# RWKV heads of a two-layer diffusion backbone: products within chunks over each head's own 64 rows, and one scan for the running sums of the decays

## The chip, the core and the metric

The kernel runs as one program on one core of a Trainium2 chip. The metric is the device time of one execution in microseconds (us), as the median of several runs. A second figure is the span of one profiled execution, from its first to its last instruction. The engines are called by the names of the profile: PE (TensorE, matrix products into PSUM), PEld (its weight loads), DVE (VectorE), ACT (ScalarE), POOL (GpSimd) and SP (the queue that issues the DMAs).

## What is computed

The reference is a backbone of two layers over 512 latent tokens and 256 context tokens, width 1024. Each layer is a mixer and an MLP with squared ReLU. The first mixer has GLA heads beside windowed attention, the second has eight RWKV-7 heads (64 wide, both directions of time) beside eight heads of latent attention (MLA). The change is in the RWKV heads of the second layer alone:

```python
def rwkv_scan(r, w, k, v, a, bb, s0):
    '''S_t = S_{t-1} (diag(w_t) + a_t b_t^T) + v_t k_t^T,  y_t = S_t r_t.'''
    def step(s, inp):
        r_t, w_t, k_t, v_t, a_t, b_t = inp
        sa = jnp.einsum('zbhij,zbhj->zbhi', s, a_t)
        s = s * w_t[..., None, :] + sa[..., :, None] * b_t[..., None, :] + v_t[..., :, None] * k_t[..., None, :]
        return s, jnp.einsum('zbhij,zbhj->zbhi', s, r_t)
...
y_ctx_d, s_ctx = rwkv_scan(*rwkv_dirs(f_ctx), s0)
y_lat_d, _ = rwkv_scan(*rwkv_dirs(f_lat), s_ctx)
```

Here f_ctx and f_lat are the features of the context and of the latents. The decay w is exp(-exp(w_log)) of a small projection; a is minus the normed key, b the normed key times a gate.

## The kernel before

**Chunks and lanes.** The kernel computes the recurrence by chunks of 64 tokens: 4 chunks of context, 8 of latents, taken in pairs p0 to p5 (p0 and p1 are the context). Everything lies by lanes: a lane is a direction and a pair of heads, so there are 8 lanes of 128 partitions, the first head on partitions 0 to 63, the second on 64 to 127 (`HALF`).

**Three stages run side by side**, as generators whose steps a plan interleaves (`plan`, L1787): `prep(p+2)` makes the operands and the products within a chunk, `inverse(p+1)` the triangular inverses, `chain(p)` the recurrence over the state. The plan's positions and priorities and the pools decide the order on each engine; each engine then works its own list in that order and waits on semaphores. Steps of `prep` for p0 and p1 stand among the MLA heads. In the trace the RWKV stage lies from 1334 to 1661 us, its pair of chunks that is looked at most closely, p4's `prep`, from 1526.40.

**prep** first makes the decays: products wz (L1549), exponentials on ACT into G, and then eight scans (L1563), one per lane, of 130 elements (two chunks of 65). The tile `reset` holds a zero at each chunk's start, so that the running sum begins anew. Per chunk, ACT makes the exponentials e1 and e3 (L1569, L1570). From these come the operands:

- AA (L1581), kk times e1, as 128x2x64 per lane: each head's rows in its own half of the columns, the other half zero (zeroed once), so that one product of 128 rows serves both heads. Four DVE writes of 64x256 a chunk.
- AC (L1585), the same values without zeros, two POOL writes of 128x256. It is transposed on PE (aT, L1601).
- BK (L1586), b and k times e3, two DVE writes of 128x512.
- RR (L1583), for latents only, r times e1 in the zero-padded form of AA: two DVE and two POOL writes of 64x256, with POOL memsets of the zero halves (L1576), since each chunk has a new RR.

The products within a chunk are gab (AA by BK, L1595), whose masked copy to GT is on DVE (L1596); the transposes aT and bkT, copied by ACT (GT L1605, BKT L1615); and for latents gmr (BK by RR, L1623), whose masked copy to GM is on DVE (L1625). Each is eight products of 128x128x128 over two PSUM banks, and each bank is copied as soon as its four products are done.

**inverse** ends in XT, which holds the inverses with zero halves, and gx (GT by XT, L1711), two banks a chunk, copied by ACT to GX (L1713).

**chain**: sa (GX by R, L1749), dS (L1760), S and R (L1763, L1765 on DVE), and for latents y, where S0 by RR (L1774) and R0 by GM (L1775) alternate into one bank.

The PSUM banks in this stage: 3 for prep (b), 2 for chain (c), 3 for inverse (i). An fp32 product shows in the trace as two hardware matmuls. Each wait is on the tile's last writer or reader.

Beside the last two recurrences run `gates` and `out1`, whose temporaries take the tags of pz (AA, G). After the stage the projection w_o follows: SP loads its weights into wraw (L335), ACT and DVE split them into whi and wlo (L322, L323), and SP also loads what the MLA heads left in DRAM (md) into the memory of actlo, and z (L1940).

Of the kernel before, what the change touches and what calls it, by code (L numbers as in the profile page):

```python
# [7 lines left out]
F32 = mybir.dt.float32  # L8
# [55 lines left out]
def _blocks(w):  # L64
    """[K, M] -> [M/128, 128 (k in tile), K/128, 128 (m in block)]"""
    k, m = w.shape
    return np.ascontiguousarray(w.reshape(k // P, P, m // P, P).transpose(2, 1, 0, 3))
# [18 lines left out]
def _rope_perm(half, reps):  # L86
    """lhsT of the signed swap: out[j] = sum_p m[p, j] x[p]; x1 rows get -x2, x2 rows get x1."""
# [12 lines left out]
class Pack:  # L100
    """columns of one [128, n] array, found by name"""
# [16 lines left out]
def prepare(i):  # L118
# [19 lines left out]
    # shape-only constants  # L138
# [20 lines left out]
    # modulation weights  # L159
    aw = i['ada_w']  # L160
    def outer(w):
        """[D, D] -> [128 (output in tile), tile, inner dimension]"""
        return w.reshape(D, KT, P).transpose(2, 1, 0)
# [5 lines left out]
    # layer 0 mixer  # L169
# [8 lines left out]
    # layer 1 mixer  # L178
# [54 lines left out]
def blocks(*ws):  # L233
    """the weights of each block of outputs, from parts of the inner dimension"""
# [3 lines left out]
class Act:  # L238
    """activations [128, KT, tokens], a tile for each part of the tokens; a slice of the tokens lies in one part"""
# [17 lines left out]
class Build:  # L257
# [6 lines left out]
    @contextmanager  # L264
    def prio(self, d):
        """what is issued inside stands d instructions later (earlier, if negative) in the scheduler's order"""
# [36 lines left out]
    def psum(self, b, s=0, **more):  # L303
        """PSUM as b single banks and s pairs of banks; more: banks of other tags. Tiles of a tag start in program
        order, so streams that run side by side have tags of their own"""
# [14 lines left out]
    def split(self, raw, hi, lo, eng=None):  # L320
        """raw = hi + lo exactly, both as float32r"""
# [3 lines left out]
    def weights(self, src, n=1024, keep=None, lead=PW):  # L325
        """one [128, n] block of weights from DRAM (or two halves of one), split"""
# [12 lines left out]
    def mm3(self, whi, wlo, ahi, alo, first, last, outs):  # L339
        """outs: list of (psum, slice of the moving operand); one k tile in three passes"""  # L340
# [8 lines left out]
    def dense(self, whi, wlo, hi, lo, nk, parts=PARTS):  # L349
        """[128 out, tokens] += w^T act; w [128, nk*128]; returns one psum tile per part"""  # L350
# [9 lines left out]
    def ada_first(self, pool, m0):  # L360
        """silu of the conditioning on all partitions, [128, stream, inner dimension]"""
# [25 lines left out]
    def ada_dot(self, pool, raw, ws, out):  # L387
        """out(w) = the weights [128, inner dimension] times the activation of stream w; raw is overwritten"""
# [4 lines left out]
    def ada_chunk(self, pool, l, j, among=False):  # L393
        """modulation part j of layer l, a tile of 128 outputs at a time: the weights with the inner dimension on
# [1635 lines left out]
```

## Time and profile before

| | |
|---|---|
| median of 3 runs | 2121.8 us (2116.98 to 2125.74) |
| span of the profiled execution | 2106.9 us |
| PE busy in it | 1976.5 us (94%) |
| DVE busy in it | 1391.4 us (66%) |
| ACT busy in it | 952.7 us (45%) |
| POOL busy in it | 308.6 us (15%) |

The profiled execution's own time isn't given beside its span; the median of the runs stands 14.9 us above the span. The shares are means over stages with different limits: most of PE's work is in the dense products of the projections and MLPs, and the share in the RWKV stage is read from that stretch alone. A busy PE is not a PE at its peak. Times in the rows are us from the span's start.

### The profile page before, as it was taken

Reading aid. Unit: us, or ns where it says so; the run is one execution under the profiler, and the core shown is the slowest. Engines: PE = TensorE matmul, PEld = TensorE weight load, DVE = VectorE, ACT = ScalarE, POOL = GpSimd, SP = SyncE. Lnnn points to the kernel's source line nnn. Section 1 sums busy time; section 2 is a strip of 40 time slices with the busy share of each in tenths; the row PEclk is TensorE's granted clock in tenths of the full one; section 3 lists DMA queues with packets and bytes.
Section 4 is the critical chain, followed back from the end, with each engine's and each line's share of the span. In section 5 each row is a group of like instructions: output and inputs, shape, how many; then the busy total and the mean of one; then the engine's idle time right before and its main releaser. Section 6 shows DMA issues by size and latency. Waiting matters only on the chain. (4 is left out here: it accounts for less than half of the span.)

```text
span 2106.9 us, 35640 instructions
## 1 busy us (share of the span) xinstructions
PE 1976.5 (94%) x14304; PEld 1643.3 (78%) x14304; DVE 1391.4 (66%) x2574; ACT 952.7 (45%) x1835; POOL 308.6 (15%) x517
## 2 busy tenths in 40 slices
PE   8998999989899999999989999978888899999998
PEld 6877666667788888888878877767677797888887
DVE  8775898736897656534484558878887555444454
ACT  5426676544622222222255646765654535333332
POOL 0003455301200000000021020033342011000001
PEclk9999799999999999999999999998999899999999
DMA  8650000053354554312243100000001412332241
GB/s 298 202 161 14 1 2 1 1 180 102 114 183 134 158 160 145 117 60 93 88 150 113 41 1 6 9 9 2 3 2 33 132 59 85 108 103 90 90 136 41
DMA packets 66282, 180.38 MB, mean 86 GB/s; under 512 B 7235, under 2 KB 12099, under 8 KB 65989
## 3 DMA queue, kind: packets, MB, share of 16 engines
q1 hardware_dynamic: 66116, 178.11, 26.4%
q8 instruction: 112, 1.84, 0.4%
q14 instruction: 54, 0.43, 0.1%
HBM read 172.57 MB, written 5.51 MB: 85 GB/s over the span
## 5 line engine op out<-in xcount | busy, mean ns | idle before, releaser
L322 ACT CAST whi<-wraw 128x1024 fp32r<-128x1024 f32 (+2 forms) x253 | 221.4, 878 | 641.2 <-PE mm L345 565.8
L343 PE MATMUL mm<-acthi,whi 128*128 128x512 f32 (+1 forms) x1464 | 443.4, 349 | 12.9 <-ACT whi L322 12.2
L347 PE MATMUL mm<-acthi,wlo 128*128 128x512 f32 (+1 forms) x1464 | 438.9, 346 | 9.3 <-DVE wlo L323 9.2
L345 PE MATMUL mm<-actlo,whi 128*128 128x512 f32 (+1 forms) x1464 | 442.2, 348 | 2.6 <-POOL actlo L1085 2.5
L323 DVE TENSOR_TENSOR wlo<-wraw,whi 128x1024 fp32r<-128x1024 f32 (+2 forms) x253 | 257.1, 1019 | 218.6 <-ACT whi L322 214.2
L343 PEld LDWEIGHTS mm<-acthi,whi 128*128 128x128 f32 x1464 | 250.7, 191 | 51.3 <-ACT whi L322 14.9
L347 PEld LDWEIGHTS mm<-acthi,wlo 128*128 128x128 f32 x1464 | 251.4, 192 | 49.0 <-DVE wlo L323 13.2
L345 PEld LDWEIGHTS mm<-actlo,whi 128*128 128x128 f32 x1464 | 251.0, 191 | 39.8 <-POOL actlo L1085 3.9
L347 PE MATMUL mm<-hh,wlo 128*128 128x512 f32 (+1 forms) x832 | 252.8, 341 | 3.6 <-DVE wlo L323 3.6
L343 PE MATMUL mm<-hh,whi 128*128 128x512 f32 (+1 forms) x832 | 253.7, 342 | 0.0
L345 PE MATMUL mm<-hl,whi 128*128 128x512 f32 (+1 forms) x832 | 253.3, 342 | 0.1
L1085 POOL TENSOR_TENSOR actlo<-lnu,acthi 128x256 fp32r<-128x256 f32 (+1 forms) x48 | 60.3, 1271 | 717.4 <-DVE lnu L1083 630.4
L347 PEld LDWEIGHTS mm<-hh,wlo 128*128 128x128 f32 x832 | 143.9, 189 | 23.2 <-DVE wlo L323 4.2
L345 PEld LDWEIGHTS mm<-hl,whi 128*128 128x128 f32 x832 | 143.6, 189 | 19.2 <-issue 0.7
L343 PEld LDWEIGHTS mm<-hh,whi 128*128 128x128 f32 x832 | 143.1, 189 | 19.5 <-issue 1.0
L1157 DVE SCALAR_TENSOR_TENSOR z<-mm,mod,z 128x512 f32<-128x512 f32 (+1 forms) x144 | 94.0, 659 | 96.6 <-PE mm L347 96.3
L391 DVE SCALAR_TENSOR_TENSOR araw<-araw,scb 128x1024 f32<-128x1024 f32 x80 | 97.8, 1222 | 56.4 <-DMA araw<-in_ada_r_dram 55.6
L1011 DVE SCALAR_TENSOR_TENSOR z<-mm,mod,z 128x256 f32<-128x256 f32 (+1 forms) x64 | 34.9, 548 | 81.2 <-PE mm L347 79.6
L322 ACT CAST hh<-relu 128x512 fp32r<-128x512 f32 (+1 forms) x100 | 50.4, 534 | 79.5 <-DVE relu L1109 79.5
L615 POOL TENSOR_TENSOR lk<-kd,Dt 64x128 f32<-64x128 f32 x144 | 74.5, 517 | 48.5 <-ACT Dt L597 20.0
L323 DVE TENSOR_TENSOR hl<-relu,hh 128x512 fp32r<-128x512 f32 (+1 forms) x100 | 56.1, 587 | 26.5 <-ACT hh L322 26.1
L391 DVE SCALAR_TENSOR_TENSOR aprod<-araw,scb 128x1024 bf16<-128x1024 f32 x48 | 58.5, 1220 | 19.6 <-DMA araw<-in_ada_r_dram 19.6
(465 smaller groups left out, 3394.0 us busy)
## 6 DMA issues: line engine op xcount, KB each, us to landing
araw<-in_ada_r_dram SPq DMA_DIRECT2D x80, 512.0 KB, 3.8
wraw<-in_w_dram SPq DMA_DIRECT2D x72, 512.0 KB, 3.5
wraw<-in_w_dram SPq DMA_DIRECT2D x144, 256.0 KB, 2.6
wraw<-in_w_s_dram SPq DMA_DIRECT2D x31, 512.0 KB, 3.6
wraw<-in_w_o_dram SPq DMA_DIRECT2D x22, 512.0 KB, 3.6
scraw<-in_ada_sc_dram SPq DMA_DIRECT2D x8, 512.0 KB, 5.3
shraw<-in_ada_sh_dram SPq DMA_DIRECT2D x8, 512.0 KB, 5.7
x<-in_xT_dram SPq DMA_DIRECT2D x8, 384.0 KB, 5.7
```

The costliest lines, as they stand in the source:

```text
L322: self.nc.scalar.copy(hi, raw)
L323: (eng or self.nc.vector).tensor_tensor(lo, raw, hi.bitcast(F32), op=ALU.subtract)
L343: mm(o, whi, ahi[:, sl], start=first, stop=False)
L345: mm(o, whi, alo[:, sl], start=False, stop=False)
L347: mm(o, wlo, ahi[:, sl], start=False, stop=last)
L391: self.nc.vector.scalar_tensor_tensor(pr, raw, 1.0, self.scb[:, w], op0=ALU.mult, op1=ALU.mult, accum_out=out(w))
L615: nc.gpsimd.tensor_tensor(K[r, :, x], kk[r, :, x], d[r, :, x], op=ALU.mult)
L1011: nc.vector.scalar_tensor_tensor(zs, o, self.mod[:, l, self.wh(i, parts), g, d:d + 1], zs, op0=ALU.mult, op1=ALU.add)
L1085: eng.tensor_tensor(lo[:, k, sl], u, hi[:, k, sl].bitcast(F32), op=ALU.subtract)
L1157: nc.vector.scalar_tensor_tensor(z[:, d, sl], o, self.mod[:, l, self.wh(i, parts), 5, d:d + 1], z[:, d, sl], op0=ALU.mult, op1=ALU.add)
```

## The change

All lines of commentary go. Line numbers shift by up to ten. What is computed differently:

- The eight scans become one over all 1040 elements of G, with `reset` as long.
- AA goes. AC is written by DVE (two writes of 128x256 a chunk) and serves gab as well as aT. RR has no zero halves: two DVE writes of 128x256, no POOL writes, no memsets. XT has no zero halves.
- gab is 16 products a chunk: for each lane and head the diagonal 64x64 tile, AC's 64 columns stationary, 128 columns of BK moving.
- gmr and gx are 16 products a chunk: 64 rows of one head, 128 stationary columns, 64 moving columns, the two heads into two banks by turns. Both banks are opened before the first product, and each is copied (GM by DVE, GX by ACT) when all have been issued.
- y first adds up all products of S0 by RR, now as 64x64 diagonal tiles, and then all of R0 by GM; the start flag stands at the first lane, the stop flag at the last.
- The temporaries of `out1` take AC's tag and not AA's; the raw tile of w_o in `gates` has 1024 columns.

```diff
-        reset = pz.tile([P, 130], F32, name="reset")
+        reset = pz.tile([P, 8 * 130], F32, name="reset")
...
-        AA = zeroed(pz, [P, 8, 2, 64], "AA")
...
-            for j in range(8):
-                gj = G[:, j].rearrange("p c t -> p (c t)")
-                nc.vector.tensor_tensor_scan(gj, reset, gj, 0.0, op0=ALU.mult, op1=ALU.add)
+            gj = G.rearrange("p j c t -> p (j c t)")
+            nc.vector.tensor_tensor_scan(gj, reset, gj, 0.0, op0=ALU.mult, op1=ALU.add)
...
-                RR = r2.tile([P, 8, 2, 64], F32, name="RR", bufs=BKB) if lat else None
-                if lat:
-                    for h in range(2):
-                        nc.gpsimd.memset(RR[HALF[h], :, 1 - h], 0.0)
+                RR = r2.tile([P, 8, 64], F32, name="RR", bufs=BKB) if lat else None
                 for d in range(2):
                     L = slice(d * 4, d * 4 + 4)
-                    for h in range(2):
-                        r = HALF[h]
-                        nc.vector.tensor_tensor(AA[r, L, h], nat('kk', d, cc)[r], e1[r, L, 0:64], op=ALU.mult)
-                        if lat:
-                            (nc.gpsimd if d else nc.vector).tensor_tensor(RR[r, L, h], nat('r', d, cc)[r], e1[r, L, 1:65],
-                                                                          op=ALU.mult)
-                    nc.gpsimd.tensor_tensor(AC[:, L], nat('kk', d, cc), e1[:, L, 0:64], op=ALU.mult)
+                    nc.vector.tensor_tensor(AC[:, L], nat('kk', d, cc), e1[:, L, 0:64], op=ALU.mult)
                     nc.vector.tensor_tensor(BK[:, L], nat('kb', d, cc),
                                             e3[:, L].unsqueeze(2).to_broadcast([P, 4, 2, 64]), op=ALU.mult)
-                kb = lambda j: BK[:, j].rearrange("p a t -> p (a t)")
+                    if lat:
+                        nc.vector.tensor_tensor(RR[:, L], nat('r', d, cc), e1[:, L, 1:65], op=ALU.mult)
+                kb = lambda j, r=slice(0, P): BK[r, j].rearrange("p a t -> p (a t)")
...
-                        mm(gp[:, u], AA[:, jb * 4 + u].rearrange("p a t -> p (a t)"), BK[:, jb * 4 + u, ::-1], start=True, stop=True)
+                        for r in HALF:
+                            mm(gp[r, u], AC[r, jb * 4 + u], BK[r, jb * 4 + u, ::-1], start=True, stop=True)
...
-                    for jb in range(2):
-                        gp = self.bank("gmr")
-                        for u in range(4):
-                            mm(gp[:, u * P:u * P + P], kb(jb * 4 + u), RR[:, jb * 4 + u].rearrange("p a t -> p (a t)"),
-                               start=True, stop=True)
-                        nc.vector.tensor_tensor(GM[:, jb * 4:jb * 4 + 4], gp.rearrange("p (j h t) -> p j h t", j=4, h=2),
-                                                self.k2('up').unsqueeze(1).unsqueeze(1).to_broadcast([P, 4, 2, 64]), op=ALU.mult)
+                    gp = [self.bank("gmr") for _ in HALF]
+                    for j in range(8):
+                        for o, r in zip(gp, HALF):
+                            mm(o[:, j * 64:j * 64 + 64], kb(j, r), RR[r, j], start=True, stop=True)
+                    for h, o in enumerate(gp):
+                        nc.vector.tensor_tensor(GM[:, :, h], o.rearrange("p (j t) -> p j t", j=8),
+                                                self.k2('up').unsqueeze(1).to_broadcast([P, 8, 64]), op=ALU.mult)
...
-                for jb in range(2):
-                    gp = self.bank("gx", "i")
-                    for u in range(4):
-                        j = jb * 4 + u
-                        mm(gp[:, u * P:u * P + P], GT[:, j, 1:3].rearrange("p a t -> p (a t)"),
-                           XT[:, c * 8 + j].rearrange("p a t -> p (a t)"), start=True, stop=True)
-                    nc.scalar.copy(GX[:, jb * 4:jb * 4 + 4].rearrange("p j h t -> p (j h t)"), gp)
+                gp = [self.bank("gx", "i") for _ in HALF]
+                for j in range(8):
+                    for o, r in zip(gp, HALF):
+                        mm(o[:, j * 64:j * 64 + 64], GT[r, j, 1:3].rearrange("p a t -> p (a t)"), XT[r, c * 8 + j],
+                           start=True, stop=True)
+                for h, o in enumerate(gp):
+                    nc.scalar.copy(GX[:, :, h], o.rearrange("p (j t) -> p j t", j=8))
...
                     for j in range(8):
-                        for h in range(2):
-                            r = HALF[h]
-                            o = yp[r, j * 64:j * 64 + 64]
-                            mm(o, S0[:, j], RR[:, j, h], start=True, stop=False)
-                            mm(o, R0[:, j, h], GM[:, j, h], start=False, stop=True)
+                        for r in HALF:
+                            mm(yp[r, j * 64:j * 64 + 64], S0[r, j], RR[r, j], start=(j == 0), stop=False)
+                    for j in range(8):
+                        for h, r in enumerate(HALF):
+                            mm(yp[r, j * 64:j * 64 + 64], R0[:, j, h], GM[:, j, h], start=False, stop=(j == 7))
...
-                    XT = zeroed(rp, [P, 16, 2, 64], "XT")
+                    XT = zeroed(rp, [P, 16, 64], "XT")
```

The order of the instructions on the engines moves with it. On DVE, the start of p4's `prep`, before: the scans, the operands of the first chunk with the recurrence's S and R between them, and the first GT.

```order
L1563 SCALAR_TENSOR_TENSOR G<-reset,G 128x130 x8
L1581 TENSOR_TENSOR AA<-fl_kk,e_14461 64x4x64
L1583 TENSOR_TENSOR RR<-fl_r,e_14461 64x4x64
L1763 TENSOR_TENSOR S<-dS,S 128x512
L1581 TENSOR_TENSOR AA<-fl_kk,e_14461 64x4x64
L1765 TENSOR_TENSOR R<-S,PC 64x8x64 x2
L1583 TENSOR_TENSOR RR<-fl_r,e_14461 64x4x64
L1586 TENSOR_TENSOR BK<-fl_kb,e_14462 128x512
L1581 TENSOR_TENSOR AA<-fl_kk,e_14461 64x4x64 x2
L1586 TENSOR_TENSOR BK<-fl_kb,e_14462 128x512
L1596 TENSOR_TENSOR GT<-gab,con_10197 128x4x128
```

The same place after. A row with x2 stands for two instructions; e is e1 or e3.

```order
L1560 SCALAR_TENSOR_TENSOR G<-reset,G 128x1040
L1573 TENSOR_TENSOR AC<-fl_kk,e_14520 128x256
L1577 TENSOR_TENSOR RR<-fl_r,e_14520 128x256
L1573 TENSOR_TENSOR AC<-fl_kk,e_14520 128x256
L1755 TENSOR_TENSOR S<-dS,S 128x512
L1574 TENSOR_TENSOR BK<-fl_kb,e_14521 128x512
L1757 TENSOR_TENSOR R<-S,PC 64x8x64 x2
L1574 TENSOR_TENSOR BK<-fl_kb,e_14521 128x512
L1577 TENSOR_TENSOR RR<-fl_r,e_14520 128x256
L1587 TENSOR_TENSOR GT<-gab,con_10197 128x4x128 x2
```

Eight operand writes and eight scans ahead of the first GT have become six writes and one scan, and the first BK, which stood behind R, stands ahead of it.

On PE, the rest of p4's first chunk, before. The order counts an fp32 product as one; xt and xn are products of the `inverse` of p3.

```order
L1595 MATMUL gab<-BK,AA 128x128 x4
L1601 MATMUL aT<-col,AC 128x128 x4
L1614 MATMUL bkT<-col,BK 128x128 x4
L1670 MATMUL xt_14700<-V,DT 32x32 x4
L1614 MATMUL bkT<-col,BK 128x128 x4
L1670 MATMUL xt_14700<-V,DT 32x32 x6
L1623 MATMUL gmr<-RR,BK 128x128 x4
L1670 MATMUL xt_14700<-V,DT 32x32 x6
L1623 MATMUL gmr<-RR,BK 128x128 x4
L1670 MATMUL xt_14700<-V,DT 32x32 x37
L1595 MATMUL gab<-BK,AA 128x128 x4
```

The same place after.

```order
L1586 MATMUL gab<-BK,AC 64x128 x8
L1592 MATMUL aT<-col,AC 128x128 x4
L1605 MATMUL bkT<-col,BK 128x128 x8
L1662 MATMUL xt_14759<-V,DT 32x32 x21
L1615 MATMUL gmr<-RR,BK 128x64 x8
L1662 MATMUL xt_14759<-V,DT 32x32 x4
L1615 MATMUL gmr<-RR,BK 128x64 x8
L1662 MATMUL xt_14759<-V,DT 32x32 x39
L1586 MATMUL gab<-BK,AC 64x128 x8
```

The second half of gmr stood behind six products of xt and each half had a copy of its own; now 16 products, with four of xt between them, end before the first copy.

On PE, the end of `inverse` for p3 and the recurrence that reads it, before.

```order
L1711 MATMUL gx<-XT,GT 128x128 x8
L1749 MATMUL sa<-R,GX 64x64 x8
L1728 MATMUL vT<-col,fl_v 64x128 x2
L1749 MATMUL sa<-R,GX 64x64 x8
L1728 MATMUL vT<-col,fl_v 64x128 x2
L1711 MATMUL gx<-XT,GT 128x128 x5
L1728 MATMUL vT<-col,vr 64x128 x4
L1711 MATMUL gx<-XT,GT 128x128 x3
L1760 MATMUL dS<-R,BKT 64x64 x16
```

The same place after.

```order
L1702 MATMUL gx<-XT,GT 128x64 x21
L1741 MATMUL sa<-R,GX 64x64
L1720 MATMUL vT<-col,fl_v 64x128 x3
L1741 MATMUL sa<-R,GX 64x64 x15
L1720 MATMUL vT<-col,fl_v 64x128
L1702 MATMUL gx<-XT,GT 128x64 x9
L1720 MATMUL vT<-col,vr 64x128 x4
L1702 MATMUL gx<-XT,GT 128x64 x2
L1752 MATMUL dS<-R,BKT 64x64 x16
```

The first chunk's gx now is 16 products, and 5 of the second chunk's stand ahead of sa; two of gx stand behind the transposes vT, right ahead of dS.

On SP, one load of wraw from w_o now stands ahead of the eight loads of md into actlo, where all six stood behind them, and two loads of z that stood behind the md loads stand ahead.

## Rows read from the trace of the kernel before

**Rows 1.** Busy time by stretch: us, engines with instructions, granted PE clock, DMA share.

```profile
1334.00:1437.00 103.00, 85.89 (x1005) 70.44 (x1003) 87.06 (x179) 67.24 (x131) 25.58 (x43) 0.92 0.03 8
...
1521.00:1564.50 43.50, 38.17 (x844) 33.31 (x843) 36.44 (x71) 24.42 (x52) 16.53 (x27) 0.92 0.01 3
```

**Rows 2.** DVE in order of time, p4's turn: start, duration, [idle before <-releaser].

```profile
1526.40 2.77 DVE L1563 TENSOR_TENSOR_SCAN G<-reset,G 128x130 f32<-128x130 f32 x8
1529.96 0.42 DVE L1581 TENSOR_TENSOR AA<-fl_kk,e 64x256 f32<-64x256 f32 x1 [0.79 <-ACT e L1569]
...
1534.73 1.42 DVE L1586 TENSOR_TENSOR BK<-fl_kb,e 128x512 f32<-128x512 f32 x1
...
1543.44 0.69 DVE L1625 TENSOR_TENSOR GM<-gmr,con 128x512 f32<-128x512 f32 x1 [0.61 <-PE gmr L1623]
...
1549.18 0.69 DVE L1596 TENSOR_TENSOR GT<-gab,con 128x512 f32<-128x512 f32 x1
...
1563.95 0.68 DVE L1763 TENSOR_TENSOR S<-dS,S 128x512 f32<-128x512 f32 x1
```

**Rows 3.** PE in order of time, the same turn.

```profile
1536.20 1.16 PE L1595 MATMUL gab<-BK,AA 128*128 128x128 f32 x8 [1.84 <-DVE BK L1586]
...
1539.25 1.06 PE L1601 MATMUL aT<-col,AC 128*128 128x128 f32 x4
...
1542.24 1.16 PE L1623 MATMUL gmr<-RR,BK 128*128 128x128 f32 x8
...
1561.72 1.15 PE L1760 MATMUL dS<-R,BKT 128*64 128x64 f32 x32
```

**Rows 4.** ACT in order of time, the same turn.

```profile
1540.35 1.50 ACT L1605 COPY GT<-aT 64x256 f32<-64x256 f32 x4 [1.96 <-PE aT L1601]
...
1542.71 1.07 ACT L1615 COPY BKT<-bkT 128x512 f32<-128x512 f32 x2
```

**Rows 5.** DVE groups, 1366 to 1660: busy us, mean ns of one, idle before.

```profile
L1581 DVE TENSOR_TENSOR AA<-fl_kk,e 64x256 f32<-64x256 f32 x32 | 17.7, 554 | 2.3 <-ACT e L1569 1.8
...
L1586 DVE TENSOR_TENSOR BK<-fl_kb,e 128x512 f32<-128x512 f32 x16 | 14.0, 873 | 0.2
L1563 DVE TENSOR_TENSOR_SCAN G<-reset,G 128x130 f32<-128x130 f32 x40 | 13.6, 416 | 2.3 <-ACT G L1559 2.3
...
L1583 DVE TENSOR_TENSOR RR<-fl_r,e 64x256 f32<-64x256 f32 x16 | 10.9, 683 | 0.1
...
L1581 DVE TENSOR_TENSOR AA<-fx_kk,e 64x256 f32<-64x256 f32 x12 | 6.4, 530 | 0.1
...
L1784 DVE TENSOR_TENSOR Y<-Y,y 128x256 f32<-128x256 f32 x8 | 3.0, 416 | 1.4 <-PE y L1775 1.3
```

**Rows 6.** POOL groups of the same stretch.

```profile
L1585 POOL TENSOR_TENSOR AC<-fl_kk,e 128x256 f32<-128x256 f32 x16 | 13.6, 858 | 2.2 <-PE aT L1601 1.8
```

**Rows 7.** PE in order of time: three shapes of product, and two shapes by turns.

```profile
1546.52 1.20 PE L1676 MATMUL xn<-DT,V 32*32 32x32 f32 x64
...
1562.80 0.70 PE L1549 MATMUL wz<-tz,con 128*128 128x256 f32 x2
1563.43 0.33 PE L1774 MATMUL y<-RR,S 128*64 128x64 f32 x2
1563.69 0.70 PE L1549 MATMUL wz<-tz,con 128*128 128x256 f32 x2
...
1567.84 1.15 PE L1749 MATMUL sa<-R,GX 128*64 128x64 f32 x31
```

**Rows 8.** PE in order of time near the start: products with two moving columns.

```profile
21.00 1.84 PE L440 MATMUL sh<-scc,shraw 128*128 128x2 f32 x16
```

**Rows 9.** All engines in order of time, the start of the w_o projection.

```profile
1661.57 3.99 SPq L1940 DMA_DIRECT2D actlo<-md  x8
...
1673.38 1.22 DVE L323 TENSOR_TENSOR wlo<-wraw,whi 128x1024 fp32r<-128x1024 f32 x1
...
1674.75 0.58 PE L343 MATMUL mm<-acthi,whi 128*128 128x256 f32 x1 [1.43 <-ACT whi L322]
```

More of the change, by code (lines that the diff above doesn't have):

```diff
@@ L1691, in inverse @@
                 b = (q % 2) * 32
-                (nc.gpsimd.tensor_copy if q < 2 else nc.scalar.copy)(XT[QD[q], :, q // 2, b:b + 32], XD[QD[q]])
+                (nc.gpsimd.tensor_copy if q < 2 else nc.scalar.copy)(XT[QD[q], :, b:b + 32], XD[QD[q]])
             yield
@@ L1700, in inverse @@
                 r = QD[2 * h]
-                nc.scalar.copy(XT[r, :, h, 32:64], g3(xo[r]))
+                nc.scalar.copy(XT[r, :, 32:64], g3(xo[r]))
             yield
@@ L1837, in gates @@
         for d, (src,) in enumerate(blocks(self.a['w1_o'])[:2]):
-            raw = rp.tile([P, 1536], F32, tag="BK", name="woraw")[:, 0:1024]
+            raw = rp.tile([P, 1024], F32, tag="BK", name="woraw")
             nc.sync.dma_start(raw, src)
@@ L1907, in layer1 @@
                 tmp = lambda tag, shape: lambda: pz.tile([P, shape], F32, tag=tag, name="g" + tag)[:, 0:512]
-                chunks = self.rwkv(pz, pools(), (self.gates(pz), self.out1(0, tmp("AA", 1024), tmp("G", 1040))))
+                chunks = self.rwkv(pz, pools(), (self.gates(pz), self.out1(0, tmp("AC", 512), tmp("G", 1040))))
                 with tc.tile_pool(name="ml", bufs=1, reuse_waits="tile") as ml:
```

## Prediction

> **What bounds the kernel now.** I first read the table of busy time by stretch [rows 1]. In the stretch from 1521.00 to 1564.50, one whole turn of the RWKV stage, PE works 38.17 of 43.50 us and VectorE 36.44: neither is full, so the turn is a chain that goes from one engine to the other, and only work on that chain counts. The rows in order of time tell which way it goes. VectorE runs the eight scans from 1526.40, ScalarE's exponentials end at 1529.96, then VectorE builds the operands until BK ends at 1536.15 [rows 2]. PE stands idle for 1.84 us until then and starts gab at 1536.20 [rows 3]. Then aT at 1539.25, its copies on ScalarE [rows 4], gmr, the second chunk's products, and the last masked copy GT at 1549.18 [rows 2]; the inverse of the next turn needs that GT, and the next scans come 45 us after these. So the operand writes of the first chunk are on the chain and those of the second (up to 1542.8) lie beside PE work.
>
> The profiled span is 2106.9 us; the median of the three runs is 2121.8. I add the difference, 14.9, to a predicted span.
>
> **Operand writes and scans.** Per chunk of latents, VectorE's four AA writes of 554 ns [rows 5] become two AC writes of 128x256, the size of the sum into Y that takes 416 ns [rows 5]; its two RR writes of 683 ns become two of 416, and GpSimd's share goes: two AC writes of 858 ns [rows 6], two of RR and two of zeros. For a pair of chunks that is VectorE 2 x (4 x 0.554 - 2 x 0.416) = 2.8 us and 2 x 2 x (0.683 - 0.416) = 1.1 us less. BK averages 873 ns, though the same shape and source took 1.42 us at 1534.73 while GpSimd was busy, and GM, of the same size, 0.69; I take 0.68 without GpSimd at its side, 4 x 0.19 = 0.8 less. Eight scans of 130 elements, 2.77 us issued one behind the other, become one of 1040. What is fixed in one scan isn't shown here: at nothing fixed it stays 2.8 us, and if all of a short scan but a rate of one 128x256 write (416 ns for 256, 1.6 ns an element) were fixed, it is 1.7. I take 2.35, the nearer to the row, so -0.4. Together -5.1 us of VectorE work in a pair, of which the first chunk's half and the scan are on the chain.
>
> Laid out from the scan's start s = 1526.40 in the order of the changed program: scan to s+2.35, exponentials, AC at s+3.1, RR, AC, the state's sum (it comes where it came, s+4.2), BK to s+5.7, the two R to about s+7.5, BK to s+8.2, and gab's second half behind it: aT at s+8.9 in place of s+12.85 [rows 3]. **Gain 3.95 us.**
>
> **The products.** For gab eight pairs of 64x64 diagonal tiles take the place of eight full products. A row of n matmuls lasts n pitches and some 0.2 us, by which the last one's record is longer. A full 128x128 product is two hardware matmuls of 0.11 us (gab: eight in 1.16 [rows 3]). Diagonal tiles run side by side: 32x32 ones of xn show 64 matmuls in 1.20 us, 16 ns each [rows 7]. So the two halves should share the time of one, and gab's PE time stays. In gmr and gx each of 16 products has 64 rows, 128 columns of weights and 64 moving columns. Moved alone, 64 columns need half of 0.11 us; the column halves of sa show 31 matmuls in 1.15 us, 31 ns each [rows 7]. The weights are the question: with two moving columns only, sixteen 128x128 matmuls take 1.84 us [rows 8], so a 128-column weight load alone is 0.10 to 0.11 us. If the two row halves load side by side, a matmul costs 0.055 and PE time stays as it is; if they don't, 0.11, and gmr and gx cost twice as much. I take 0.055, since the 32-row strips of xn seem to load theirs side by side (below, B), and keep the other end below.
>
> In y the S0 products become 64x64 diagonals and stand ahead of the R0 products. The alternation of two products in y runs at some 30 ns a matmul now, so nothing is won there, and between full-size products it costs: wz 0.70, y 0.33, wz again start 0.89 us apart [rows 7], some 0.35 above the work of both. The changed order has gab cut once into y, and 37 such changes of shape in a pair against 38: nothing.
>
> **What is given back.** gmr now opens two banks before its first product, and its sixteen products must end before either GM can start. The stage has three banks for these tags. The second gmr bank is the one that the first BKT copy leaves, at t0+4.0 (t0 is aT's start; BKT at 1542.71, half of 1.07 us [rows 4]). So gmr starts at t0+4.1 instead of t0+3.0, takes 32 x 0.055 plus a piece of xt and two changes of shape, 2.45 us, and ends at t0+6.55, where the second GM of before could start at t0+5.5. Both GM, both BK, DT, GT and two DT stand behind it on VectorE, the waiting engine: 8 operations of 0.6 to 0.7 us put the last GT at t0+11.6; before it stood at t0+9.93 [rows 2, 3]. **Loss 1.65 us.**
>
> gx has the same form: both copies GX come after all sixteen products. sa and dS then stand 0.9 us later, and dS ended at 1562.87 while S waited for VectorE until 1563.95 [rows 2, 3]: 1.1 us of cover, so nothing; without it, 0.9 a chunk.
>
> So a pair of latent chunks gains 3.95 - 1.65 = 2.3, and the four of them 9.2. **The context pairs** run among MLA heads, where PE is busy 85.89 of 103.00 us [rows 1]: VectorE saves 4 x (4 x 0.530 - 2 x 0.416) = 5.2 us there (AA from fx_kk [rows 5]) and 0.8 in scans; I take half of it on the path, -2.9, and +1.0 for gab's pieces among full-size products (nine places, 0.35 each, a third on the path): -1.9. **The tail** of the last pair has one gx with nothing beside it: +0.5.
>
> **The loads at the end.** Before, eight actlo loads of md wait on SP's queue until 1661.57 for VectorE's last read of the temporary beneath them, and the w_o weights stand behind them [rows 9]. In the changed layout they lie elsewhere: the order has the first w_o load ahead of the md loads, and none of them waits for that read any more. It is worth nothing, since PE's idle 1.43 us at 1674.75 ends with VectorE's wlo, which stands at 1673.38 behind Y's gating and the sum into z of the block before [rows 9]; if PE waits for the load alone, 2 us go.
>
> **Sum:** -9.2 - 1.9 + 0.5 = -10.6, a span of 2096.3 and **2111.2 us**. Its own range is 2103 to 2120: all of the context savings (3), a scan of 1.7 (2.6) and the loads (2) make it 8 less; no context gain (1.9) and no cover for gx (4 x 2 x 0.9) make it 9 more.
>
> **Rivals.** (B, slower) The halves' weights load one after the other: 0.11 us a matmul [rows 8]. gmr then takes 32 x 0.055 = 1.8 us more a chunk, all of it ahead of GM and, in the second chunk, of gx; gx takes 1.8 more a chunk, against which 0.2 of cover is left. A pair goes from -2.3 to -2.3 + 4 x 1.8 - 0.2 = +4.7, the four to +18.8, the tail to 0.5 + 3.6; with -1.9 that is +21, **2143**. It decides from about 73 ns a matmul, where a third of these 32 us uses up the gain of 10.6. For it: the weights are 128 columns wide, whatever the rows. The Trainium skill ("TensorE: Matmul & The Clock Gate", LDWEIGHTS) says that a weight load takes time by columns and not by rows, which by itself would give this. Against it stand the 16 ns of the 32-row strips [rows 7]: a load of 32 columns, a quarter of 0.10 us, would take 26 ns, and loads one after the other wouldn't fit. The same page (Part 3, The mechanism) lets a load overlap a running matmul when the row groups differ, which is the case here.
>
> (C, larger gain) PE's clock: the mean granted in the turn is 0.92 and in the first stretch too [rows 1], so the lower level, 1.2 GHz, was granted in some 16% of the time, 7 us of a turn; ahead of gab PE had stood idle for 1.84 us [rows 3]. With gab 4 us earlier some of that goes, and if GM's delay meets idle time, the loss above goes too: 1.65 x 4 + 2 = 9 more, **2102**, at best 2095.
>
> (D, no change) The 64x64 diagonals don't run side by side: gab's 32 half matmuls a chunk cost 0.11 us each and not 0.055, 1.6 us more after the overlap at their ends, and a pair's gain of 2.3 becomes a loss of 0.9: 4 x 0.9 - 1.9 + 0.5 = +2, **2124**. Against it: the strips of xn.
>
> **How the numbers follow.** Forecast 0.50, B 0.20, C 0.20, D 0.10. Forecast is 2111; the range reaches from 2096 (C) to 2139 (most of B); it leaves out C's end and B's upper half. Half a per cent, 10.6 us, is about what a measurement of this kernel can tell from no change; the forecast lies on that bound. Faster: C and nearly half of the forecast, 0.42. Same: the rest of the forecast and D with a little of B, 0.38. Slower: B, 0.20.
>
> **What would show it.** One scan row of 2.2 to 2.5 us; AC at 0.42 and BK at 0.68; first gab 5.7 us after the scan's start, aT 9 after it; gmr 1.8 us for 32 matmuls (B: 3.5); last GT 11.6 after aT; dS done before S is free for it; scans 42 to 43 us apart instead of 45. It would be wrong if gmr or gx take over 75 ns a matmul, if y's split costs a clock fall, or if the period of the scans is held by the inverse alone and doesn't move.

## The result, and the profile after

The changed kernel takes 2140.9 us (median of four runs, 2128.42 to 2149.73); the kernel before, timed with it, takes 2122.7 (four runs, 2116.98 to 2125.74). The ratio is 1.0101, with a 95% interval of 1.0073 to 1.0129: slower by 1.0%. The forecast was 2111.2, faster by 0.5%; the range ended at 2139.0.

The profiled execution of after has a span of 2133.7 us and a mean granted clock of 0.953. I cut both traces at the same events: the start of the first pair's scans, that of the third pair's (p2), that of the last (p5), and the first product of w_o. The first stretch is the context's, among the MLA heads; the second holds three turns of the latents; the third the last turn and the tail. Columns are as in [rows 1]. Before:

```profile
1334.08:1441.78 107.70, 88.72 (x1041) 72.78 (x1039) 89.34 (x183) 70.06 (x135) 26.62 (x44) 0.91 0.03 8
1441.78:1571.35 129.57, 109.28 (x2363) 94.53 (x2361) 111.87 (x219) 75.68 (x160) 48.24 (x75) 0.92 0.01 3
1571.35:1662.89 91.54, 79.40 (x1618) 63.06 (x1619) 59.55 (x120) 42.01 (x79) 20.23 (x29) 0.90 0.14 40
```

After:

```profile
1341.58:1455.31 113.73, 99.71 (x1180) 79.20 (x1181) 84.16 (x161) 69.56 (x136) 15.32 (x29) 0.85 0.03 7
1455.31:1593.58 138.27, 127.24 (x2619) 109.88 (x2605) 101.53 (x186) 73.64 (x157) 26.08 (x45) 0.86 0.01 2
1593.58:1687.86 94.28, 84.74 (x1754) 68.83 (x1755) 56.57 (x109) 43.72 (x82) 12.69 (x19) 0.89 0.21 62
```

The stage grew from 328.8 to 346.3 us, by 17.5, which is about the whole difference of the medians (18.2). One profiled execution of each is not a sharp measure, though: their spans differ by 26.8 us, and 7.5 of these lie ahead of the stage, where nothing was changed. POOL's and DVE's work shrank in all three stretches, as the change says (DVE 111.87 to 101.53 in the three turns). PE's grew from 109.28 to 127.24 us there, and its granted clock fell from 0.92 to 0.86; in the context stretch it fell from 0.91 to 0.85. So the time came in on PE, by work and by clock. The context stretch has no gmr, and e1 and e5 below, with the same products in it, run it in 108.50 and 107.34 us; so some 5 of its 113.73 us are chance of this one execution, and the three turns are the part to read.

p4's turn, engine by engine. DVE in order of time, the answer to [rows 2]:

```profile
1547.83 2.33 DVE L1560 TENSOR_TENSOR_SCAN G<-reset,G 128x1040 f32<-128x1040 f32 x1 [0.58 <-ACT G L1557]
1550.92 0.42 DVE L1573 TENSOR_TENSOR AC<-fl_kk,e 128x256 f32<-128x256 f32 x1 [0.77 <-ACT e L1566]
...
1552.54 0.68 DVE L1574 TENSOR_TENSOR BK<-fl_kb,e 128x512 f32<-128x512 f32 x1
...
1569.78 0.69 DVE L1587 TENSOR_TENSOR GT<-gab,con 128x512 f32<-128x512 f32 x1 [0.52 <-PE gab L1586]
1575.67 1.97 DVE L1631 STREAM_TRANSPOSE X<-TA 128x1024 f32<-128x1024 f32 x1 [5.20 <-PE x L1690]
```

PE in order of time, the answer to [rows 3], with gmr of both chunks and gx:

```profile
1553.31 1.09 PE L1586 MATMUL gab<-BK,AC 64*64 64x128 f32 x16
...
1556.43 0.66 PE L1592 MATMUL aT<-col,AC 128*128 128x128 f32 x4
...
1559.25 2.00 PE L1615 MATMUL gmr<-RR,BK 64*128 64x64 f32 x16 [0.30 <-ACT GT L1596]
...
1561.37 2.00 PE L1615 MATMUL gmr<-RR,BK 64*128 64x64 f32 x16
...
1564.09 1.90 PE L1586 MATMUL gab<-BK,AC 64*64 64x128 f32 x16
1565.92 1.91 PE L1668 MATMUL xn<-DT,V 32*32 32x32 f32 x64
...
1575.46 2.05 PE L1615 MATMUL gmr<-RR,BK 64*128 64x64 f32 x30
...
1577.52 2.84 PE L1702 MATMUL gx<-XT,GT 64*128 64x64 f32 x40
...
1582.30 1.77 PE L1702 MATMUL gx<-XT,GT 64*128 64x64 f32 x18
```

And the same turn cut into four stretches, columns as in [rows 1]:

```profile
1547.83:1559.25 11.42, 9.90 (x237) 7.94 (x237) 10.57 (x16) 7.60 (x18) 3.67 (x7) 1.00 0.01 3
1559.25:1564.20 4.95, 4.95 (x120) 4.73 (x122) 2.41 (x5) 1.85 (x4) 0.00 (x0) 1.00 0.00 0
1564.20:1574.40 10.20, 10.20 (x178) 9.08 (x180) 3.84 (x6) 4.25 (x9) 2.00 (x4) 0.50 0.01 3
1574.40:1593.58 19.18, 18.84 (x410) 16.04 (x408) 16.77 (x37) 11.55 (x25) 2.96 (x4) 1.00 0.01 3
```

The first half of the turn went as predicted: AC 3.1 us after the scan's start, the first BK done at 5.4, aT at 8.6 (12.85 before). Then three things are to be seen. gmr of the first chunk is two rows of 16 matmuls with 2.00 us each, 115 ns from start to start (a single record of this shape lasts 0.27 us, which is taken off for the last one); in the second chunk 30 matmuls take 2.05 us, 61 ns. From 1559.25 on PE has no idle time, 4.95 of 4.95 us and 10.20 of 10.20. In the kernel before, too, it had next to none behind aT; it waited ahead of it, as the same turn shows there (scan to aT, and from aT to behind the last GT):

```profile
1526.40:1539.25 12.85, 8.75 (x186) 7.89 (x183) 11.89 (x23) 5.22 (x11) 7.67 (x12) 0.82 0.01 1
1539.25:1553.00 13.75, 13.42 (x356) 11.89 (x355) 9.38 (x15) 7.57 (x18) 4.84 (x10) 0.92 0.02 4
```

So PE's work behind aT had little room to grow. And from 1564.20 for 10.2 us the granted clock is 0.50, the lower of the two levels (1.2 GHz), with PE busy without a gap ahead of it: gab takes 1.90 us there and 1.09 at 1553.31. VectorE now waits 5.20 us for PE ahead of X.

Why 115 and 61 ns: the order of the changed program, with the numbers of the tiles, which the words of the plain order hide.

```order
L1615 MATMUL gmr_14653<-RR_14526,BK_11885 128x64 x8
L1662 MATMUL xt32_14759<-V_14744,DT_14676 32x32 x4
L1615 MATMUL gmr_14654<-RR_14526,BK_11885 128x64 x8
```

The two numbers are the two banks, one for each head. The loop writes the heads by turns, but when it comes up the second bank isn't free, and in the order that is built all of the first head stands ahead of all of the second; it is so in the first chunk of all four latent pairs. In the second chunks the heads alternate, in p3 from the first product on, in the others behind three to five products of each head.

### The profile page after: what moved, and what is told of

Read it like the earlier page. It is cut to its first block, busy times and chain, and to the rows that moved or that the text cites. A ratio compares the mean times of both kernels' runs of the same rounds, so it can differ in the third digit from the quotient of the medians.

```text
span 2133.7 us, 36522 instructions
## 1 busy us (share of the span) xinstructions
PE 2018.6 (95%) x14816; PEld 1675.7 (79%) x14816; DVE 1374.4 (64%) x2508; ACT 951.9 (45%) x1835; POOL 265.5 (12%) x460
## 4 chain that ended last, share of the span: by engine, by line
PE 75%; DVE 13%; ACT 5%; DMA 4%; issue 3%; POOL 1%; DVEq 0%; SPq 0%; ACTq 0%; POOLq 0%
PE mm L345 17%; PE mm L347 17%; PE mm L343 16%; DMA araw<-in_ada_r_dram 3%; PE var L1053 2%; PE go L786 2%; PE ms L1435 1%; DVE wlo L323 1%; PE gx L1702 1%; PE gab L1586 1%; PE gmr L1615 1%; PE lev L660 1%; DVE z L1069 1%; PE st L1479 1%; DVE araw L391 1%
```

## Experiments

The theories. **T1**: the loss comes from products of half of the rows that don't alternate: they take 0.11 us and not 0.055, and PE's clock falls behind them. **T2**: the tiles of 64 rows lower the clock as such, alternating or not. **T3**: the place of gmr behind bkT is what costs. **T4**: gx carries the loss. **T5**: any longer gmr lowers the clock through the waits of others. All runs, with the stage measured as above in the one profiled execution, the granted clock in the three turns of its middle stretch, and the ratio to the kernel before from the timed runs:

```
kernel                              stage us  clock  median us  ratio to before (95%)
before                              328.8     0.92
after                               346.3     0.86   2140.9     1.0101 (1.0073 to 1.0129)
e1  gmr ahead of bkT                321.8     0.96   2117.8     0.9993 (0.9964 to 1.0021)
e2  full gmr                        -         -      2116.7     0.9984 (0.9957 to 1.0011)
e3  full gmr and gx                 314.4     0.97   2091.7     0.9878 (0.9855 to 0.9902)
e4  writes alone                    317.1     0.94   2093.6     0.9895 (0.9865 to 0.9926)
e5  e1, one head after the other    355.2     0.85   2162.6     1.0211 (1.0169 to 1.0253)
e6  e1 with gx of before            320.7     0.92   2105.8     0.9946 (0.9922 to 0.9971)
e7  after with gx of before         334.9     0.87   2118.1     1.0018 (1.0001 to 1.0036)
e8  before with gmr ahead of bkT    328.2     0.89   2119.6     1.0019 (1.0000 to 1.0038)
e9  e1, full gmr issued twice       342.8     0.96   2120.4     1.0009 (0.9980 to 1.0038)
e10 put together                    312.6     0.97   2101.4     0.9905 (0.9876 to 0.9934)
```

The kernel before took 2116.7 to 2120.4 us in the median beside these. The profile of e2, with a span of 4758.8 us, can't be set beside the others, so e2 gave times only. Single stages carry chance of some us: in e1 the stage says 7 us less than before, the runs say 1. e2, e3, e4 and e9 compute other numbers than the reference; e10, which has the reference's, has the same clock in the turns as e3 (0.97).

**e1: gmr ahead of the transposes bkT.**

```diff
+                GM = None
+                if lat: ...        # gmr and its two masked copies
                 BKT = rp.tile([P, 8, 2, 64], F32, name="BKT", bufs=BKB)
...
-                GM = None
-                if lat: ...
```

> The changed kernel with one move: the block of gmr and its two masked copies stands ahead of the transposes bkT, so that both of its banks are free when it begins and the two heads' products can alternate. In the trace of the changed kernel the gmr of each pair's first chunk is not alternating: all 16 matmuls of one head, then the 16 of the other, 1.72 us each at the upper clock (115 ns a matmul), while the second chunk of p4, which alternates, takes 2.00 us for 32 (64 ns). In the four latent turns the lower clock is granted within 0.2 to 5 us behind the one-headed gmr (1472.0, 1516.4, 1564.2, 1608.6). T1: the loss comes from halves that do not alternate, in gmr and in the clock behind it. Then gmr falls to about 1.8 us in the first chunks, 4 x 1.7 = 7 us go, and the low clock in the stage falls from 99 us towards the 68 us of the kernel before, worth up to another 8: 10 to 15 us below the changed kernel, near 2128, that is within 0.5 per cent of the kernel before. T2: the clock is lowered by 64-row tiles as such (gab, y), alternating or not; then gmr is shorter, but the low clock stays near 99 us and only 4 to 7 us go, near 2135.

PE in order of time, gmr of p4's first and second chunk:

```profile
1545.51 2.59 PE L1608 MATMUL gmr<-RR,BK 64*128 64x64 f32 x32
...
1555.98 2.00 PE L1608 MATMUL gmr<-RR,BK 64*128 64x64 f32 x32
```

The context stretch and the three turns, columns as in [rows 1]:

```profile
1344.64:1453.14 108.50, 94.83 (x1178) 74.68 (x1180) 83.97 (x160) 69.29 (x136) 15.17 (x29) 0.91 0.03 8
1453.14:1577.71 124.57, 111.76 (x2657) 95.19 (x2642) 101.40 (x186) 75.58 (x159) 26.70 (x45) 0.96 0.01 3
```

All 32 of the second chunk take 2.00 us, 56 ns a matmul; the first chunk has four products of each head ahead that don't alternate and takes 2.59 us, not 4.1. The clock is 0.96, above the kernel before, and the lower level was granted for 37.5 us in the stage (summed over the records of the granted clock), 93 in after and 60 in before. 24.5 us of the stage are gone, 5.2 of them in the context stretch, which has no gmr, and 13.7 in the three turns; the kernel ties with the one before, more than T1 expected. T2 falls: gab and y are the same 64-row tiles here, and the clock doesn't mind.

**e2 and e3: gmr, and gmr and gx, as full products.**

```diff
-                            mm(o[:, j * 64:j * 64 + 64], kb(j, r), RR[r, j], start=True, stop=True)
+                            mm(gp[:, u * P:u * P + P], kb(j), rr[:, k0:k0 + P], start=True, stop=True)
```

(rr is RR as 512 columns, k0 the lane's first; gx in the same way over XT.)

> The changed kernel with gmr as eight products of 128x128x128 a chunk again, four to a bank, each bank copied after its four, over the same RR without zeros: the moving operand is two lanes of RR, so that GM holds other numbers (what is computed is changed there). T1: gmr's first chunk takes 0.88 us a bank as before, GM no longer waits for 16 products, 1.7 us and the wait of 1.65 us go in each of four turns, and the low clock behind gmr goes: 12 to 18 us below the changed kernel, near 2126. T2: 7 us for gmr, the low clock stays at 85 to 99 us in the stage: near 2134.

> As the run with full gmr, and gx as eight products of 128x128x128 a chunk as well, its moving operand two units of XT (GX and all behind it hold other numbers). In the changed kernel gx takes 2.79 + 1.50 + 0.17 us for two chunks in p4's turn against 1.75 + 1.00 + 0.56 before, and its low-clock stretches lie in the context turns. T1: another 1.1 us a turn, of which the state's sum covers some, 2 to 6 us below the run with full gmr alone, near 2122, as the kernel before or a little under it. T2: the low clock stays, near 2131.

e2 came out 25 us below the changed kernel by the ratios, more than the 12 to 18 expected. e3 is faster than the kernel before by 1.2%, and again 1.1% below e2, more than the 2 to 6 us expected: the form of gx costs on the path, which the prediction had put at nothing.

**e4: the writes alone.** gab and y, too, in the form of before.

> The DVE part of the change alone: one scan, AC and RR without zeros written once by DVE, no POOL writes and no memsets, while gab, gmr, gx and y have the forms of the kernel before (128 rows, y's two products alternating) over the same tiles without zeros. The numbers in GT, GM, GX and y are others than the reference's, and e3 is made smaller by a constant factor to keep them finite. The prediction's DVE part was worth 3.95 us to the first aT in each latent turn and 2.9 us in the context turns: 4 x 3.95 + 2.9 = 18.7 us under the kernel before if all of it counts, near 2104; if the inverse holds the turn's period, near 2122. T1 expects it 5 us or more under the kernel before (no unalternated halves, no further clock falls); T2 as well. If it is as slow as the changed kernel, both are wrong and the loss lies in the writes.

0.9895, the stage 11.7 us shorter. The part of the change that is on DVE and POOL does what it was predicted to do, at 11.7 us of stage (some 22 by the ratio) where 18.7 was the most expected; gab's diagonals and y's new order add nothing that can be seen (e3 and e4 have overlapping intervals).

**e5: one head after the other, at e1's place.** This is the direct test.

```diff
-                    for j in range(8):
-                        for o, r in zip(gp, HALF):
+                    for o, r in zip(gp, HALF):
+                        for j in range(8):
                             mm(o[:, j * 64:j * 64 + 64], kb(j, r), RR[r, j], start=True, stop=True)
```

> The run with gmr ahead of bkT, with one edit: all eight products of the first head are written ahead of the eight of the second, so that nothing alternates, at the same place and with the same banks. T1 (the alternation is what counts): gmr takes 115 ns a matmul, 3.5 us a chunk against 2.3 to 2.9 in the first and 1.73 in the second chunks, some 3 us more a latent turn, 12 in the four, and the low clock in the stage, 37.5 us with gmr ahead, comes back to 60 to 100 us within 5 us behind gmr: stage (first scan to the first w_o product) of 335 to 350 us against 321.8, time 2130 to 2142. T3 (the place of gmr ahead of bkT is what counts): stage within 3 us of 321.8, low clock near 40 us, time near 2118.

PE, gmr of p4's two chunks:

```profile
1555.03 3.39 PE L1608 MATMUL gmr<-RR,BK 64*128 64x64 f32 x32
...
1565.83 3.39 PE L1608 MATMUL gmr<-RR,BK 64*128 64x64 f32 x32
```

The context stretch, the three turns, and the last turn with the tail:

```profile
1341.58:1448.92 107.34, 93.42 (x1179) 73.84 (x1180) 84.00 (x160) 69.29 (x136) 15.18 (x29) 0.92 0.03 8
1448.92:1588.27 139.35, 129.69 (x2656) 112.83 (x2642) 100.81 (x187) 75.02 (x159) 25.51 (x45) 0.85 0.01 2
1588.27:1696.79 108.52, 98.96 (x1727) 80.31 (x1718) 56.67 (x109) 42.49 (x80) 14.20 (x19) 0.76 0.17 51
```

The same products on the same tiles in another order: 100 ns a matmul instead of 56 to 75, the clock down from 0.96 to 0.85, the stage 33 us longer, the ratio 1.0211. That is more than T1 had (335 to 350 us of stage, 2130 to 2142 of time). The clock isn't lower in the profiled execution alone: over the whole program it was 0.933 to 0.948 in the executions behind e5's ratio and 0.952 to 0.972 in e1's. But the lower level doesn't follow every time: behind both chunks of p4, shown above, none was granted until 1600.6. The place is the same as in e1, so T3 falls; e8 agrees, where the same move in the kernel before changes nothing.

> The kernel before with one move: its block of gmr (full products) stands ahead of bkT. It shows what the place alone is worth. T1: little, since gmr's banks were copied after four products each and its products took 0.88 us a bank: stage within 4 us of 328.8, time within 0.3 per cent of the kernel before. T3: as much as the same move gave the changed kernel, 24 us of stage: near 305 us and 2095.

**e9: as long, but with all rows.** gmr as full products, each issued twice, at e1's place: the PE time of e5 without half-used rows.

> The run with gmr ahead of bkT, with gmr as full 128x128x128 products, each issued twice: 32 matmuls of 111 ns a chunk, 3.5 us, the same PE time as the run with one head after the other, but with all rows of the array in use. The moving operand is two lanes of RR, so GM and what follows hold other numbers. It parts what one head after the other does: T1 (matmuls that use half of the rows, one at a time, lower the clock): here the clock stays, 35 to 60 us low in the stage, and the stage grows over 321.8 by the PE time alone, 1.2 to 1.75 us in each of eight chunks, to 325 to 333 us; time 2115 to 2128. T5 (a longer gmr makes others wait, and the idle time behind it lowers the clock, whatever the rows): 90 us low or more, stage near 350 us, time 2145 or more.

```profile
1552.00 3.84 PE L1612 MATMUL gmr<-RR,BK 128*128 128x128 f32 x32
...
1563.12 3.73 PE L1612 MATMUL gmr<-RR,BK 128*128 128x128 f32 x32
```

```profile
1456.40:1585.72 129.32, 117.54 (x2656) 103.12 (x2642) 101.50 (x186) 74.93 (x159) 26.60 (x45) 0.96 0.01 3
1585.72:1687.91 102.19, 91.34 (x1732) 73.75 (x1719) 56.44 (x109) 42.38 (x80) 13.23 (x19) 0.83 0.21 62
```

3.84 and 3.73 us, longer than e5's 3.39, and yet the clock in the three turns stays at 0.96 and these take 129.32 us, against 139.35 in e5 and 124.57 in e1. So it isn't the time that gmr takes: with matmuls on half of the rows, one at a time, the lower clock comes in most turns, and with the same time on all rows it doesn't. The table parts the same way: the clock in the turns is 0.85 to 0.87 in the three kernels with gmr one head after the other (after, e5, e7) and 0.89 to 0.97 in all others. e9's copies start after half of the products, e5's after all of them; e1's wait for all, too, with the clock at 0.96, so the copies alone don't lower it. T5 falls in the turns. In the tail T1 missed: there this execution had the lower clock for 34 us, from 1639.6, where no gmr is left (PE had stood idle for 1.27 us ahead of 1638.30), and so its stage was 342.8 and not 325 to 333; the median of its runs, 2120.4, is where T1 had it. What lowers the clock in the tail stays open; e5's last stretch, at 0.76, has it as well.

**e6 and e7: gx in the form of before**, with XT's zero halves back, in e1 and in the changed kernel.

> The run with gmr ahead of bkT, and gx in the form of the kernel before: XT with zero halves, eight products of 128x128x128 a chunk, each bank copied after its four; the result is the reference's. If the form of gx costs on the path what PE shows (2.84 + 1.50 + 0.17 us for a turn's two chunks against 1.75 + 1.00 + 0.56, 1.2 us a turn, and copies that wait for all 16), the stage falls from 321.8 to 314 to 317 us and the time to 2105 to 2113, faster than the kernel before. If the state's sum covers it, as the prediction took it, the stage stays at 320 to 323 and the time at 2115 to 2119.

> The changed kernel with gx alone back in the form of the kernel before (XT with zero halves); gmr stays as changed, behind bkT and not alternating in the first chunks. T1: gmr and the clock behind it carry most of the loss, so the stage falls from 346.3 to 338 to 343 us and the low clock in it stays above 80 us; time near 2134. T4 (gx carries the loss: 25 us lay between the runs with full gmr and with full gmr and gx): the stage falls below 330 us and the time to about 2118.

e7's three stretches:

```profile
1338.80:1446.66 107.86, 90.55 (x1105) 71.13 (x1103) 84.14 (x161) 69.39 (x135) 16.08 (x28) 0.92 0.03 8
1446.66:1583.92 137.26, 126.31 (x2582) 108.87 (x2579) 102.33 (x187) 74.60 (x159) 27.42 (x45) 0.87 0.01 2
1583.92:1673.71 89.79, 78.87 (x1659) 63.35 (x1655) 56.87 (x109) 42.58 (x81) 13.68 (x19) 0.94 0.23 71
```

Taking gx back gave 11.4 us of stage in the changed kernel, between T1 and T4, and 0.8% of the time, where T4 had it (2118): it alone brings the changed kernel back to the kernel before, as moving gmr alone does (e1). So each form carries about half of the 2% that lie between the writes alone (e4) and the changed kernel. In e1 taking gx back gave 0.5%, though only 1 us of that profiled stage, whose clock was lower (0.92). Where gx's half comes in is less clear. Its order is like gmr's: in a turn's second chunk five products of one head, then five of the other, and only then by turns; 88 ns a matmul at 1582.30 above. But its clock isn't: e7's turns, with gmr as in the changed kernel and the old gx, stay at 0.87 and are 1.0 us shorter, and e1's, with the new gx, are at 0.96. 5.9 of the 11.4 us lie in the context stretch, which e1 and e5 run as fast with the new gx. And e6 and e7 give back two things at once, the full products and the copy after every four of them; no run changes gx's order alone. So the alternation is shown as the cause for gmr and only argued for gx.

**e10: put together.** One scan, AC by DVE and gab's diagonals from the changed kernel; gx, gmr and y in the form of before; RR with zeros, by four DVE operations with a factor for each partition.

```diff
+                        for h in range(2):
+                            nc.vector.scalar_tensor_tensor(RR[:, L, h], nat('r', d, cc), hm[:, h:h + 1], e1[:, L, 1:65],
+                                                           op0=ALU.mult, op1=ALU.mult)
```

> A version put together from what the runs showed, with the reference's result: one scan, AC by DVE and gab as diagonal tiles as in the changed kernel; gx and XT, gmr and y in the form of the kernel before; RR with zero halves, written by four DVE operations of 128x256 a chunk (r times e1 times a factor of 1 or 0 for each partition), without POOL writes and memsets. From the run with full gmr and gx (stage 314.4 us, 2091.7) and two more DVE writes of 0.42 to 0.48 us a chunk, of which the first chunk's lie ahead of the recurrence's R: stage 316 to 320 us, low clock 35 to 55 us, time 2093 to 2101, ratio 0.988 to 0.993. If alternation had nothing to do with it, it would be as slow as the changed kernel.

```profile
1340.22:1445.71 105.49, 90.18 (x1105) 71.71 (x1103) 84.16 (x160) 69.49 (x135) 16.26 (x28) 0.91 0.04 8
1445.71:1565.90 120.19, 106.17 (x2465) 89.55 (x2462) 103.03 (x199) 74.82 (x159) 26.86 (x45) 0.97 0.01 3
1565.90:1652.77 86.87, 74.89 (x1647) 59.28 (x1646) 57.36 (x113) 42.41 (x80) 13.83 (x19) 0.95 0.20 59
```

PE, aT and gx of p4's turn (its scan starts at 1524.72):

```profile
1534.58 0.66 PE L1598 MATMUL aT<-col,AC 128*128 128x128 f32 x4
...
1550.44 2.02 PE L1709 MATMUL gx<-XT,GT 128*128 128x128 f32 x16 [0.47 <-ACT XT L1699]
```

0.9905: 1% faster than the kernel before and 2% faster than the changed one. The three turns take 120.19 us, 129.57 before.

## Why the prediction was wrong

**The step that failed is gmr's duration, and with it the clock.** "gmr ... takes 32 x 0.055 plus a piece of xt and two changes of shape, 2.45 us" rests on the heads alternating. The price of an alternating matmul was right: 56 ns in e1. But in the first chunk of each pair they don't alternate, and it took 4.1 us in p4 (1559.25 to 1563.37). The fence that stood ahead of the prediction shows it, x8, four of xt, x8, and the text read the two eights as a cut through alternating products. The same paragraph held the reason: the second bank comes free only with the first BKT copy. It should have followed that the head whose bank is free comes first. gmr ended at t0+6.9 all the same (6.55 predicted), by luck: its first head started at t0+2.8 and not at t0+4.1. The prediction's own sign of being wrong, gmr over 75 ns a matmul, came.

**The larger part is the clock behind it, which the forecast had as unchanged** and rival C as a gain. In p4 the last GT came at t0+13.35, and PE's gab and xn ahead of it took 1.90, 1.91 and 1.97 us at the lower level; at 1.09, 1.20 and 1.09, their upper-level rows, it would by estimate have stood near t0+11, no later than the predicted 11.6. Over the stage the lower level went from 60 us to 93, and 37.5 in e1; at half the clock the 55 us more of it than in e1 are up to 28 us of PE time (an estimate), and the stage is 24.5 longer than e1's.

**gx: "so nothing"** was wrong as well. The cover of 1.1 us was counted for later copies only, not for matmuls at 88 ns and not for PE having become the bound of the turn, 43.90 of p4's 45.75 us (39.28 of 44.95 before), where little is covered any more. Measured, the form of gx costs 0.5 to 1.1% of the time (e6, e7, e3); by which of its parts stays open.

**Rival B** gave 2143, and the measurement is 2140.9, but not by its mechanism, so that its number is luck: it had the halves' weight loads follow each other always. The matmuls run side by side when the heads alternate (56 ns), and when they don't they cost the 0.11 us that a load alone takes in the products with two moving columns [rows 8]. The Trainium skill's sentence that a load overlaps a running matmul only when the row groups differ ("TensorE: Matmul & The Clock Gate", Part 3, The mechanism) fits both: within one head the row group is the same. The trace agrees with it (56 ns by turns, 115 within one head); what was missing was to ask which order the matmuls come in. B also left out the clock and the context pairs' gx, and had 7.2 us a turn of PE time where PE's work grew by 6 us a turn, clock and all (127.24 - 109.28 over three). The range ended 2 us below the measurement.

**What was right.** The groups of DVE over the latent chunks, the answers to [rows 5]:

```profile
L1574 DVE TENSOR_TENSOR BK<-fl_kb,e 128x512 f32<-128x512 f32 x16 | 11.0, 685 | 3.3 <-PE gmr L1615 3.2
...
L1577 DVE TENSOR_TENSOR RR<-fl_r,e 128x256 f32<-128x256 f32 x16 | 10.8, 676 | 0.0
...
L1573 DVE TENSOR_TENSOR AC<-fl_kk,e 128x256 f32<-128x256 f32 x16 | 8.3, 520 | 2.3 <-ACT e L1566 2.3
```

BK 685 ns (0.68 predicted, 873 before), AC 520 and RR 676, where 416 was taken: some of these writes are longer than others, as RR's 1.26 us at 1555.28, with POOL at work on S; the cause wasn't tried. The scan takes 2.33 us in p4 (2.35 predicted). aT came at 8.6 after the scan's start (8.9 predicted). Without the PE forms the DVE part is worth what the sum gave it: e10's turns are 3.1 us shorter in the mean (9.4 over three), where the sum had 3.95 less what is given back, and its context stretch 2.2 us shorter (1.9 predicted). gab's diagonals do run side by side, 55 ns a half (1.09 us for 16): rival D is out. The loads at the end were worth nothing, as predicted:

```profile
1680.58 4.57 SPq L1933 DMA_DIRECT2D actlo<-md  x8
...
1697.47 0.28 PE L343 MATMUL mm<-acthi,whi 128*128 128x256 f32 x1
...
1698.85 1.22 DVE L323 TENSOR_TENSOR wlo<-wraw,whi 128x1024 fp32r<-128x1024 f32 x1
...
1700.12 0.39 PE L347 MATMUL mm<-acthi,wlo 128*128 128x256 f32 x1 [2.25 <-DVE wlo L323]
```

The first w_o load now goes ahead of the md loads at 1680.58, whi's product runs at 1697.47, and PE then waits 2.25 us for VectorE's wlo.

**The 14.9 us** between span and median were no fixed addition: for the changed kernel time and span of one execution lie 1.8 us apart. The profiled execution of before was one of its quicker ones, so its stage, not its whole span, was the thing to build on.

## What to carry to other kernels

Where products on different rows of the array are to run side by side, they must be neighbours in the order that is issued, and every bank that they write must be free when the first of them starts; look at the order with the tiles' numbers, since equal names hide which half comes when. A half-filled array can cost twice: here its matmuls took twice as long each, and the clock fell behind them in most turns and slowed everything else on the engine. A form that saves writes can be taken apart from the form of the products that it makes possible: here the writes alone were worth 1%, and the other forms of the products took 2% back.

## What the runs showed of the hardware

- Matmuls with 64 rows, 128 weight columns and 64 moving columns (fp32, two to a product): 56 ns each when two row halves alternate (e1), 100 to 115 ns when all of one half come ahead of the other (e5, after).
- PE's granted clock fell to the lower level behind such one-sided matmuls although PE hadn't been idle (10.2 us from 1564.20 in after), though not every time (not behind p4's in e5); with all rows in use for as long (e9) it stayed at 0.96 in the turns, against 0.85 in e5.
- One scan of 1040 elements takes 2.33 us in p4, eight of 130 take 2.77, so by estimate some 0.06 us is fixed in each of them; VectorE's BK write of 128x512 took 873 ns in the mean with POOL's AC and RR writes beside it and 685 without them.
